# Row means on one core: the wait for the last store moved behind the closing barriers, waits reordered, and rows in three parts

## Chip, cores and metric

One core of a Trainium2 chip. The metric is the time of one execution in device microseconds (us). The span of a profile is the stretch from the kernel's first to its last instruction on any engine; the timed run is longer than its span.

## The reference

```python
batch, seq, dim = 32, 512, 1024          # x: float32, 67.1 MB
def reference(x, divisor):               # divisor = 1024.0
    return (np.sum(x, axis=-1) / divisor).astype(np.float32)
```

16,384 rows of 1,024 floats, one mean for each. On 128 partitions that makes 128 rows per partition.

## The kernel before

The rows lie in two parts. Of the first, each partition has 120 rows that follow one another in memory (so the next partition's block starts 480 KB further on); of the second, 8 rows (32 KB further on). The parts set which means go out with which store.

```python
L = 8
M = J - L                                                # 120
x_main = bass.AP(tensor=x.tensor, offset=0, ap=[[M * D, P], [D, M], [1, D]])
x_last = bass.AP(tensor=x.tensor, offset=P * M * D, ap=[[L * D, P], [D, L], [1, D]])
...
main = [(14, 0)] * 6 + [(14, 4), (14, 6), (8, 4)]        # (rows of a load, of them on ScalarE)
last = [(4, 2), (2, 1)]                                  # then one row, and one row in three pieces
bulk = ctx.enter_context(tc.tile_pool(name="bulk", bufs=3))
...
for rows, on_act in main:
    t = bulk.tile([P, 14, D], F32, name="t")
    load(t[:, :rows, :], x_main[:, j : j + rows, :])     # SyncE's queue
    sums(res[:, j : j + rows], t, rows, on_act)          # VectorE, a few rows on ScalarE
    j += rows
```

The last row is read in pieces pa, pb and pc, so that little arithmetic is left after the last byte:

```python
act_sum(pc[:, D - b : D - b + 1], pa)                    # ScalarE
nc.vector.reduce_sum(out=pc[:, D - b + 1 :], in_=pb, axis=AX)
nc.vector.reduce_sum(out=q[:, L - 1 :], in_=pc, axis=AX)
nc.vector.scalar_tensor_tensor(out=fin, in0=q, scalar=scale, in1=r, op0=MULT, op1=ADD)
tc.keep_in_program_order(nc.sync.dma_start(out=o_last, in_=fin))     # the last store
```

Behind it the program closes: SyncE waits for every engine and every DMA, and then all engines go through two barriers with a clearing of the semaphores between them.

Of the kernel before, what the change touches and what calls it, by code (L numbers as in the profile page):

```python
# [1 line left out]

# [4 lines left out]

F32 = mybir.dt.float32
ADD = mybir.AluOpType.add
MULT = mybir.AluOpType.mult  # L10
COPY = mybir.ActivationFunctionType.Copy
AX = mybir.AxisListType.X


def start_loads_at_once(nc):



    sp = mybir.EngineType.SP
    first, body = nc.main_func.blocks[0], nc.main_func.blocks[1]  # L20
    loads = []
    for i in body.instructions:
        if i.engine == sp:
            if type(i).__name__ != "InstDMACopy" or (i.sync_info and i.sync_info.on_wait):
                break
            loads.append(i)
    names = {i.name for i in loads}
    assert names
    body.instructions = [i for i in body.instructions if i.name not in names]
    at = next(  # L30
        k for k, i in enumerate(first.instructions) if i.engine == sp and type(i).__name__ == "InstDrain"
    )
    first.instructions = first.instructions[:at] + loads + first.instructions[at:]


@with_exitstack
def kernel(
    ctx: ExitStack,
    tc: tile.TileContext,
    x: bass.AP,  # L40
    divisor: float,
    out: bass.AP,
):
    nc = tc.nc
    nc.at_finalize(start_loads_at_once)
    xf = x.flatten_outer_dims()
    N, D = xf.shape
    P = nc.NUM_PARTITIONS
    scale = 1.0 / float(divisor)
    J = N // P  # L50
    assert J * P == N


    L = 8
    M = J - L
    x_main = bass.AP(tensor=x.tensor, offset=0, ap=[[M * D, P], [D, M], [1, D]])
    x_last = bass.AP(tensor=x.tensor, offset=P * M * D, ap=[[L * D, P], [D, L], [1, D]])
    o_main = bass.AP(tensor=out.tensor, offset=0, ap=[[M, P], [1, M]])
    o_last = bass.AP(tensor=out.tensor, offset=P * M, ap=[[L, P], [1, L]])


    main = [(14, 0)] * 6 + [(14, 4), (14, 6), (8, 4)]
    last = [(4, 2), (2, 1)]
    assert sum(n for n, _ in main) == M and sum(n for n, _ in last) == L - 2
    bulk = ctx.enter_context(tc.tile_pool(name="bulk", bufs=3))
    one = ctx.enter_context(tc.tile_pool(name="one", bufs=1))
    psum = ctx.enter_context(tc.tile_pool(name="junk", bufs=4, space=bass.MemoryType.PSUM))

    res = one.tile([P, M], F32, name="res")
    fin = one.tile([P, L], F32, name="fin")  # L70
    q = one.tile([P, L], F32, name="q")
    r = one.tile([P, L], F32, name="r")
    nc.gpsimd.memset(r, 0.0)  # L73

    def load(dst, src):
        tc.keep_in_program_order(nc.sync.dma_start(out=dst, in_=src))  # L76

    def act_sum(dst, src, by=1.0):
        n = src.shape[-1]
        junk = psum.tile([P, D], F32, name="junk")  # L80
        nc.scalar.activation(junk[:, :n], src, COPY, scale=by, accum_out=dst)  # L81

    def sums(dst, t, rows, on_act):
        d = rows - on_act
        for i in range(d, rows):
            act_sum(dst[:, i : i + 1], t[:, i, :])
        nc.vector.reduce_sum(out=dst[:, :d], in_=t[:, :d, :], axis=AX)  # L87

    j = 0
    for rows, on_act in main:  # L90
        t = bulk.tile([P, 14, D], F32, name="t")
        load(t[:, :rows, :], x_main[:, j : j + rows, :])
        sums(res[:, j : j + rows], t, rows, on_act)
        j += rows
    j = 0
    for rows, on_act in last:
        t = one.tile([P, rows, D], F32, name=f"t{rows}")
        load(t, x_last[:, j : j + rows, :])
        sums(q[:, j : j + rows], t, rows, on_act)
        j += rows  # L100


    c = 768
    row = one.tile([P, D], F32, name="row")
    load(row, x_last[:, j, :])
    act_sum(r[:, j : j + 1], row[:, c:], by=scale)
    nc.vector.reduce_sum(out=q[:, j : j + 1], in_=row[:, :c], axis=AX)  # L107



    a, b = 448, 704
    pa = one.tile([P, a], F32, name="pa")
    pb = one.tile([P, b - a], F32, name="pb")
    pc = one.tile([P, D - b + 2], F32, name="pc")
    load(pa, x_last[:, L - 1, :a])
    load(pb, x_last[:, L - 1, a:b])
    load(pc[:, : D - b], x_last[:, L - 1, b:])


    nc.gpsimd.tensor_scalar_mul(out=res, in0=res, scalar1=scale)  # L120
    tc.keep_in_program_order(nc.sync.dma_start(out=o_main, in_=res))

    act_sum(pc[:, D - b : D - b + 1], pa)
    nc.vector.reduce_sum(out=pc[:, D - b + 1 :], in_=pb, axis=AX)  # L124
    nc.vector.reduce_sum(out=q[:, L - 1 :], in_=pc, axis=AX)  # L125
    nc.vector.scalar_tensor_tensor(out=fin, in0=q, scalar=scale, in1=r, op0=MULT, op1=ADD)  # L126
    tc.keep_in_program_order(nc.sync.dma_start(out=o_last, in_=fin))


# [1 line left out]
_INS = ['x', 'divisor']  # L131
_OUTS = [((32, 512), 'float32')]

_NUMBERS = {'divisor': 1024.0}


# [26 lines left out]
```

## Time and profile before

| | |
|---|---|
| timed, median of 3 runs | 162.98 us (medians of five later sets: 162.89 to 163.01) |
| span of the profiled run | 161.51 us (its own time 163.29) |
| DMA engines full | 97.1% of the span |
| VectorE busy | 74% |
| first load's landing | 19.90 us |
| VectorE's last instruction ends | 159.14 us |
| last store's landing | 160.58 us |

The prediction below shows the lines of the page, of the stretches and of the end. How to read them: a stretch line has the window, then each engine's busy time with its number of instructions, then the DMA share and GB/s; a timeline line has start, duration, engine, line, operation and shapes. The closing itself can be seen in the view of the line that all closing instructions carry. Its columns are line, engine's queue, instruction and count, duration in ns (least, median, most), first and last start:

```profile
L158 SPq EVENT_SEMAPHORE  x7: 17/28/912, 159.6 to 161.4; - x7
L158 PEldq EVENT_SEMAPHORE  x2: 51/51/51, 161.0 to 161.5; - x2
```

SyncE stands for 912 ns in one wait (for the store's landing); only then TensorE's queue, which like all has one wait per barrier, passes the first at 161.0 and the second at 161.5.

### The profile page before, as it was taken

To read this page: it belongs to the slowest core of one execution; us is meant where nothing else is said; L and a number is where in the kernel's file an instruction comes from. 1 tells how busy PE (TensorE), PEld (TensorE's weight loads), DVE (VectorE), ACT (ScalarE), POOL (GpSimd) and SP (SyncE) were. 2 spreads that over 40 slices of the span, in tenths; PEclk is the share of its full clock that TensorE was granted. 3 is DMA by queue.
4 is the path that set the end of the run, shared out by engine and by line. 5 is a ranking of instruction groups with operands and counts; after the bars stand their busy time and mean duration, and the time that the engine had idled before them with its cause. 6 is when DMAs were issued, how large, how long until landed. Compare 5 with 4: busy or idle time off the path is not lost.

```text
span 161.5 us, 138 instructions
## 1 busy us (share of the span) xinstructions
DVE 120.0 (74%) x15; ACT 20.7 (13%) x39; POOL 0.8 (0%) x6
## 2 busy tenths in 40 slices
DVE  0000099968998699959995999599968970697893
ACT  3000000000000000000000000000008100682881
POOL 0000000000000000000000000000000000000100
DMA  9999999999989999999999899999999978999990
GB/s 298 398 440 454 454 454 454 454 440 440 412 355 398 454 454 454 454 454 454 440 440 412 355 398 454 454 454 454 454 454 440 440 327 383 487 414 394 410 384 6
DMA packets 2448, 67.18 MB, mean 416 GB/s; under 512 B 528, under 2 KB 912, under 8 KB 1040
## 3 DMA queue, kind: packets, MB, share of 16 engines
q1 hardware_dynamic: 2448, 67.18, 97.1%
HBM read 67.11 MB, written 0.07 MB: 416 GB/s over the span
## 4 chain that ended last, share of the span: by engine, by line
DMA 67%; DVE 29%; another core or an unknown queue 1%; SPq 1%; issue 0%; DVEq 0%
DMA t<-in_x_dram 45%; DVE res L87 28%; DMA row<-in_x_dram 22%; SPq L76 1%; DVE q L107 1%; DVE q L125 0%; DVE pc L124 0%; DVE fin L126 0%; DVEq L125 0%; DVEq L126 0%
## 5 line engine op out<-in xcount | busy, mean ns | idle before, releaser
L87 DVE TENSOR_REDUCE res<-t 128x14 f32<-128x14336 f32 (+3 forms) x9 | 114.4, 12716 | 38.2 <-DMA t<-in_x_dram 38.2
L81 ACT ACTIVATE junk<-t 128x1024 f32<-128x1024 f32 x17 | 17.2, 1013 | 135.6 <-DMA t<-in_x_dram 135.6
L87 DVE TENSOR_REDUCE q<-t 128x2 f32<-128x2048 f32 (+1 forms) x2 | 3.5, 1752 | 0.7 <-DMA t<-in_x_dram 0.7
L81 ACT ACTIVATION_READ_ACCUMULATOR junk<-t 128x1 f32 x17 | 3.2, 188 | 0.0
L81 ACT ACT_TABLE_LOAD x1 | 1.3, 1283 | 1.7 <-PEq L144 1.7
L120 POOL TENSOR_SCALAR res<-res 128x120 f32<-128x120 f32 x1 | 0.5, 513 | 151.0 <-DVE res L87 151.0
L107 DVE TENSOR_REDUCE q<-row 128x1 f32<-128x768 f32 x1 | 1.0, 953 | 0.1
L125 DVE TENSOR_REDUCE q<-pc 128x1 f32<-128x322 f32 x1 | 0.5, 489 | 0.1
L81 ACT ACTIVATE junk<-pa 128x448 f32<-128x448 f32 x1 | 0.5, 547 | 0.1
L124 DVE TENSOR_REDUCE pc<-pb 128x1 f32<-128x256 f32 x1 | 0.4, 420 | 0.0
L81 ACT ACTIVATE junk<-row 128x256 f32<-128x256 f32 x1 | 0.4, 388 | 0.2 <-DMA row<-in_x_dram 0.2
L126 DVE SCALAR_TENSOR_TENSOR fin<-q,r 128x8 f32<-128x8 f32 x1 | 0.2, 167 | 0.1
L81 ACT ACTIVATION_READ_ACCUMULATOR junk<-row 128x1 f32 x1 | 0.2, 188 | 0.0
L81 ACT ACTIVATION_READ_ACCUMULATOR junk<-pa 128x1 f32 x1 | 0.2, 185 | 0.0
L73 POOL MEMSET r<- 128x8 f32 x1 | 0.1, 105 | 1.3 <-POOLq L144 1.3
L144 POOL MEMSET const-bfloat16-1.0<- 128x1 bf16 x1 | 0.1, 102 | 0.0
L144 POOL MEMSET const-uint8-127<- 128x1 uint8 x1 | 0.1, 102 | 0.0
L144 POOL MEMSET const-float32-0.0<- 128x1 f32 x1 | 0.1, 99 | 0.2 <-issue 0.2
L144 POOL MEMSET const-float32-1.0<- 128x1 f32 x1 | 0.1, 100 | 0.0
## 6 DMA issues: line engine op xcount, KB each, us to landing
t<-in_x_dram SPq DMA_DIRECT2D x8, 7168.0 KB, 35.7
t<-in_x_dram SPq DMA_DIRECT2D x1, 4096.0 KB, 28.5
t<-in_x_dram SPq DMA_DIRECT2D x1, 2048.0 KB, 33.0
t<-in_x_dram SPq DMA_DIRECT2D x1, 1024.0 KB, 35.0
row<-in_x_dram SPq DMA_DIRECT2D x1, 512.0 KB, 35.9
pa<-in_x_dram SPq DMA_DIRECT2D x1, 224.0 KB, 36.0
pc<-in_x_dram SPq DMA_DIRECT2D x1, 160.0 KB, 35.7
pb<-in_x_dram SPq DMA_DIRECT2D x1, 128.0 KB, 35.8
```

What stands on the lines that cost most here:

```text
L73: nc.gpsimd.memset(r, 0.0)
L76: tc.keep_in_program_order(nc.sync.dma_start(out=dst, in_=src))
L81: nc.scalar.activation(junk[:, :n], src, COPY, scale=by, accum_out=dst)
L87: nc.vector.reduce_sum(out=dst[:, :d], in_=t[:, :d, :], axis=AX)
L107: nc.vector.reduce_sum(out=q[:, j : j + 1], in_=row[:, :c], axis=AX)
L120: nc.gpsimd.tensor_scalar_mul(out=res, in0=res, scalar1=scale)
L124: nc.vector.reduce_sum(out=pc[:, D - b + 1 :], in_=pb, axis=AX)
L125: nc.vector.reduce_sum(out=q[:, L - 1 :], in_=pc, axis=AX)
L126: nc.vector.scalar_tensor_tensor(out=fin, in0=q, scalar=scale, in1=r, op0=MULT, op1=ADD)
L144: nc = _bacc.Bacc("TRN2", target_bir_lowering=False, num_devices=1)
```

## The change

Three things. The last store is taken out of the body and put behind the wait that collects everything else, but ahead of the barriers; SyncE waits for its landing as the very last thing (with a semaphore of its own, which the clearing leaves alone). The prediction calls this "store behind the barriers"; it is the wait for the landing that goes behind them. Where an instruction waits for several semaphores, the one expected last is kept on the instruction itself. And the rows lie in three parts of 56, 56 and 16 rows per partition, so that a partition's block is 224 KB or 64 KB from the next; the first part's means get a store of their own in the middle of the loads.

```diff
+def latest_wait_first(nc):
+    def rank(i, w):
+        own = {"DVE": "DVE_", "Activation": "Activation_", "SP": "DVE_", "Pool": "DVE_"}
+        if w.ant_name.startswith("DMAHW") and i.engine != SP:
+            return 0
+        return 1 if w.ant_name.startswith(own.get(str(i.engine).split(".")[-1], "?")) else 2
+    ...                                   # sorts the waits of each body instruction by rank
+def close_while_storing(nc, landed):
+    ...
+    needs[lane.id] = ...                  # the collected wait no longer counts the last store
+    del needs[done.id]                    # nor VectorE's last instruction
+    last = nc.sync.wait_ge(landed, 16).ins
+    body.instructions = [i for i in body.instructions if i.name != store.name]
+    end.instructions = [
+        with_sync(drain, on_wait=tuple(needs.values())),
+        with_sync(store, on_wait=(done,), on_update=(add,)),
+        *end.instructions[1:-1],          # the two barriers and the clearing
+        with_sync(last, on_update=(sub,)),
+    ]
...
-    L = 8
-    M = J - L
+    B, L = 56, 16
...
-    main = [(14, 0)] * 6 + [(14, 4), (14, 6), (8, 4)]
-    last = [(4, 2), (2, 1)]
+    main = [[(14, 0)] * 4, [(14, 0)] * 2 + [(14, 4), (14, 6)]]
+    last = [(8, 4), (4, 2), (2, 1)]
...
+            if k == 1 and j == B:
+                means_out(0)              # scale and store the first part's means
```

More of the change, by code (lines that the diff above doesn't have):

```diff
@@ L1 @@
+import copy
+import dataclasses
 from contextlib import ExitStack
@@ L12 @@
 AX = mybir.AxisListType.X
+SP = mybir.EngineType.SP
 def start_loads_at_once(nc):
-    sp = mybir.EngineType.SP
     first, body = nc.main_func.blocks[0], nc.main_func.blocks[1]
@@ L22, in start_loads_at_once @@
     for i in body.instructions:
-        if i.engine == sp:
+        if i.engine == SP:
             if type(i).__name__ != "InstDMACopy" or (i.sync_info and i.sync_info.on_wait):
@@ L30, in start_loads_at_once, with with_sync @@
     at = next(
-        k for k, i in enumerate(first.instructions) if i.engine == sp and type(i).__name__ == "InstDrain"
+        k for k, i in enumerate(first.instructions) if i.engine == SP and type(i).__name__ == "InstDrain"
     )
     first.instructions = first.instructions[:at] + loads + first.instructions[at:]
+def with_sync(i, on_wait=None, on_update=None):
+    s = i.sync_info
+    return copy.replace(
+        i,
+        sync_info=mybir.SyncInfo(
+            on_wait=s.on_wait if on_wait is None else on_wait,
+            on_update=s.on_update if on_update is None else on_update,
+        ),
+    )
@@ new lines, in latest_wait_first @@
+def latest_wait_first(nc):
[4 more added lines that the diff above has]
+        return 1 if w.ant_name.startswith(own.get(str(i.engine).split(".")[-1], "?")) else 2
+    for block in nc.main_func.blocks[1:2]:
+        block.instructions = [
+            with_sync(i, on_wait=tuple(sorted(i.sync_info.on_wait, key=lambda w: rank(i, w))))
+            if i.sync_info and len(i.sync_info.on_wait) > 1
+            else i
+            for i in block.instructions
+        ]
@@ new lines, in close_while_storing @@
+def close_while_storing(nc, landed):
+    body, end = nc.main_func.blocks[1], nc.main_func.blocks[-1]
+    store = [i for i in body.instructions if i.engine == SP and type(i).__name__ == "InstDMACopy"][-1]
+    (lane,) = store.sync_info.on_update
+    drain = end.instructions[0]
+    assert drain.engine == SP and type(drain).__name__ == "InstDrain"
+    needs = {w.id: w for w in drain.sync_info.on_wait}
+    assert needs[lane.id].wait_value > lane.update_value
+    needs[lane.id] = dataclasses.replace(
+        needs[lane.id], wait_value=needs[lane.id].wait_value - lane.update_value
+    )
+    (done,) = [w for w in store.sync_info.on_wait if w.ant_name.startswith("DVE_")]
+    assert needs[done.id].wait_value == done.wait_value
+    del needs[done.id]
+    own = dict(sync_type="semaphore", id=landed.num, ant_name=landed.name)
+    add = mybir.SyncUpdate(update_mode="sem-add-imm", update_value=16, **own)
+    sub = mybir.SyncUpdate(update_mode="sem-sub-imm", update_value=16, **own)
+    last = nc.sync.wait_ge(landed, 16).ins
+    assert nc.main_func.blocks[-1].instructions[-1].name == last.name
+    body.instructions = [i for i in body.instructions if i.name != store.name]
[4 more added lines that the diff above has]
+        with_sync(last, on_update=(sub,)),
+    ]
@@ L44 @@
     nc = tc.nc
+    landed = nc.alloc_semaphore("landed")
     nc.at_finalize(start_loads_at_once)
+    nc.at_finalize(latest_wait_first)
+    nc.at_finalize(lambda nc: close_while_storing(nc, landed))
     xf = x.flatten_outer_dims()
@@ L51, with part @@
     assert J * P == N
-    L = 8
-    M = J - L
-    x_main = bass.AP(tensor=x.tensor, offset=0, ap=[[M * D, P], [D, M], [1, D]])
-    x_last = bass.AP(tensor=x.tensor, offset=P * M * D, ap=[[L * D, P], [D, L], [1, D]])
-    o_main = bass.AP(tensor=out.tensor, offset=0, ap=[[M, P], [1, M]])
-    o_last = bass.AP(tensor=out.tensor, offset=P * M, ap=[[L, P], [1, L]])
-    main = [(14, 0)] * 6 + [(14, 4), (14, 6), (8, 4)]
-    last = [(4, 2), (2, 1)]
-    assert sum(n for n, _ in main) == M and sum(n for n, _ in last) == L - 2
+    B, L = 56, 16
+    assert 2 * B + L == J
+    def part(t, first, n, width):
+        cols = [[width, n], [1, width]] if width > 1 else [[1, n]]
+        return bass.AP(tensor=t.tensor, offset=first * P * width, ap=[[n * width, P]] + cols)
+    x_part = [part(x, 0, B, D), part(x, B, B, D), part(x, 2 * B, L, D)]
+    o_part = [part(out, 0, B, 1), part(out, B, B, 1), part(out, 2 * B, L, 1)]
+    main = [[(14, 0)] * 4, [(14, 0)] * 2 + [(14, 4), (14, 6)]]
+    last = [(8, 4), (4, 2), (2, 1)]
+    assert all(sum(n for n, _ in m) == B for m in main) and sum(n for n, _ in last) == L - 2
     bulk = ctx.enter_context(tc.tile_pool(name="bulk", bufs=3))
@@ L67 @@
     psum = ctx.enter_context(tc.tile_pool(name="junk", bufs=4, space=bass.MemoryType.PSUM))
-    res = one.tile([P, M], F32, name="res")
+    res = [one.tile([P, B], F32, name=f"res{k}") for k in range(2)]
     fin = one.tile([P, L], F32, name="fin")
@@ L87, in sums, with means_out @@
         nc.vector.reduce_sum(out=dst[:, :d], in_=t[:, :d, :], axis=AX)
-    j = 0
-    for rows, on_act in main:
-        t = bulk.tile([P, 14, D], F32, name="t")
-        load(t[:, :rows, :], x_main[:, j : j + rows, :])
-        sums(res[:, j : j + rows], t, rows, on_act)
-        j += rows
+    def means_out(k):
+        nc.gpsimd.tensor_scalar_mul(out=res[k], in0=res[k], scalar1=scale)
+        tc.keep_in_program_order(nc.sync.dma_start(out=o_part[k], in_=res[k]))
+    for k in range(2):
+        j = 0
+        for rows, on_act in main[k]:
+            t = bulk.tile([P, 14, D], F32, name="t")
+            load(t, x_part[k][:, j : j + rows, :])
+            sums(res[k][:, j : j + rows], t, rows, on_act)
+            j += rows
+            if k == 1 and j == B:
+                means_out(0)
     j = 0
     for rows, on_act in last:
-        t = one.tile([P, rows, D], F32, name=f"t{rows}")
-        load(t, x_last[:, j : j + rows, :])
+        if rows == 8:
+            t = bulk.tile([P, 14, D], F32, name="t")[:, :8, :]
+        else:
+            t = one.tile([P, rows, D], F32, name=f"t{rows}")
+        load(t, x_part[2][:, j : j + rows, :])
         sums(q[:, j : j + rows], t, rows, on_act)
@@ L104 @@
     row = one.tile([P, D], F32, name="row")
-    load(row, x_last[:, j, :])
+    load(row, x_part[2][:, j, :])
     act_sum(r[:, j : j + 1], row[:, c:], by=scale)
@@ L114 @@
     pc = one.tile([P, D - b + 2], F32, name="pc")
-    load(pa, x_last[:, L - 1, :a])
-    load(pb, x_last[:, L - 1, a:b])
-    load(pc[:, : D - b], x_last[:, L - 1, b:])
-    nc.gpsimd.tensor_scalar_mul(out=res, in0=res, scalar1=scale)
-    tc.keep_in_program_order(nc.sync.dma_start(out=o_main, in_=res))
+    load(pa, x_part[2][:, L - 1, :a])
+    load(pb, x_part[2][:, L - 1, a:b])
+    load(pc[:, : D - b], x_part[2][:, L - 1, b:])
+    means_out(1)
     act_sum(pc[:, D - b : D - b + 1], pa)
@@ L126 @@
     nc.vector.scalar_tensor_tensor(out=fin, in0=q, scalar=scale, in1=r, op0=MULT, op1=ADD)
-    tc.keep_in_program_order(nc.sync.dma_start(out=o_last, in_=fin))
+    tc.keep_in_program_order(nc.sync.dma_start(out=o_part[2], in_=fin))
 _INS = ['x', 'divisor']
```

## The prediction

> **What bounds the kernel now.** The kernel sums 16,384 rows of 1,024 floats, so it reads 67.1 MB and does one pass of adds. I read the head of the page first (who is busy), then the stretches of the run (is the transfer rate steady), then the chain and the timeline of the last microseconds, then what SyncE's queue waits for at the end.
>
> The page, busy shares and DMA queue:
>
> ```profile
> DVE 120.0 (74%) x15; ACT 20.7 (13%) x39; POOL 0.8 (0%) x6
> ...
> q1 hardware_dynamic: 2448, 67.18, 97.1%
> ```
>
> The 16 DMA engines are 97.1% full, and VectorE has a quarter of the span free. Stretches of one load each (columns: from:to, length, DVE, ACT, POOL, clock, DMA share, GB/s):
>
> ```profile
> 20.00:37.00 17.00, 15.18 (x2) 0.00 (x0) 0.00 (x0) 1.00 1.00 432
> 37.00:54.00 17.00, 15.14 (x2) 0.00 (x0) 0.00 (x0) 1.00 1.00 432
> 105.00:122.00 17.00, 15.14 (x2) 0.46 (x1) 0.00 (x0) 1.00 1.00 432
> 122.00:138.50 16.50, 10.37 (x2) 3.81 (x8) 0.00 (x0) 1.00 0.98 421
> 138.50:158.30 19.80, 17.97 (x6) 15.14 (x30) 0.51 (x1) 1.00 0.95 400
> ```
>
> Every stretch moves 432 GB/s until the short pieces of the end. (The coarse strip of 40 slices wavers between 355 and 454 only because a 57,344-byte packet falls into one slice or the next.) In the trace's packets, one of 57,344 bytes takes 2,116 ns at the median, so 16 engines move 16 x 57,344 / 2,116 = 433.6 GB/s. The exception is the first packet of each engine: 2,333 to 3,552 ns. The slowest engine finishes its first one at 4.76 us, and seven more at 2.116 us each end at 19.6, which agrees with the first landing at 19.90. The loads then land at 36.81, 53.76 and so on, 16.94 us apart (8 x 2.116 = 16.93). So what the slowest engine loses in its first packet is never won back, and afterwards nothing is lost.
>
> The end, timeline from 156.5 us:
>
> ```profile
> 156.93 0.95 DVE L107 TENSOR_REDUCE q<-row 128x1 f32<-128x768 f32 x1
> 157.87 0.42 DVE L124 TENSOR_REDUCE pc<-pb 128x1 f32<-128x256 f32 x1
> 158.07 0.18 ACT L81 ACTIVATION_READ_ACCUMULATOR junk<-pa 128x1 f32 x1
> 158.38 0.49 DVE L125 TENSOR_REDUCE q<-pc 128x1 f32<-128x322 f32 x1
> 158.98 0.17 DVE L126 SCALAR_TENSOR_TENSOR fin<-q,r 128x8 f32<-128x8 f32 x1
> 159.17 0.34 SPq L127 DMA_DIRECT2D out_dram<-fin  x1
> ```
>
> and what SyncE waits for after it, with the time of that store to landing:
>
> ```profile
> SPq L158 <- DMA out_dram<-fin: 0.9, 1, 0.9
> ```
> ```profile
> out_dram<-fin SPq DMA_DIRECT2D x1, 4.0 KB, 1.4
> ```
>
> The last piece pc lands at 158.25; VectorE ends pb's sum at 158.29 and ScalarE pa's at 158.25, so three legs meet. The store is issued at 159.17 and its last semaphore increment comes at 160.58. Only then does SyncE go through its remaining waits and the two closing barriers, to the end at 161.51. The tail from 158.25 to 161.51 is 3.26 us: 0.92 arithmetic, 1.41 store, 0.93 closing.
>
> **What the Trainium skill says.** "DMA: Bandwidth & Descriptors", section Specifications, gives 435 GB/s as the fabric ceiling; the 433.6 above agrees, so the steady state has no headroom for a new address pattern to win. The same page, "Latency and other measured facts", row "HBM row pitch at large powers of two", tells of pitches of 512 KiB and more that slow copies (207 GB/s at 512 KiB, 103 at 4 MiB); the 480 KB pitch of this kernel shows no such loss after the first packets, and 224 and 64 KB are not in its list. The same page's "Anatomy of one DMA" puts most of a small DMA's fixed time of about 2 us into the receipt of the write, not the moving; here the 4 KB store needs 1.41 us although its packets take 7 to 9 ns each, so it is latency that other work can cover. "Perfetto Trace Analysis", section Identifying Dependency Chains, says that an instruction with several waits may have semaphore instructions put before it; the trace has such a one at 158.28 ahead of the reduction of pc and at 158.91 ahead of the last multiply-add.
>
> **The change part by part.** From the built order of both kernels: the loads keep number, sizes and order; VectorE and ScalarE have the same instructions on the same shapes (fin is 16 wide in place of 8). Four things differ.
>
> 1. *Store behind the barriers.* SyncE makes its collected waits first, without VectorE's last and without this store; then it issues the store, takes part in both barriers, and waits for the landing last. Are its collected waits met in time? The last are pc's landing (158.25) and the landing of the store of the earlier means (158.50 in the trace); some waits at about 0.06 us each (159.56, 159.62, 159.69 are the starts of three in a row) follow, so SyncE is ready near 158.8, before VectorE's end at 159.14. After the issue at 159.17 + 0.34 = 159.51 the barriers take what they take now, from SyncE's drain at 160.76 to 161.51, 0.75 us: to about 160.3. The landing at 160.58 is later and decides; with some 0.05 us for the wait itself the end is at 160.63. Saved: 161.51 - 160.63 = 0.88 us.
>
> 2. *Order of waits.* The instruction now keeps the wait expected last and the others stand in the one before it. For the reduction of pc, all three legs end within 0.04 us and the separate instruction still has VectorE's and ScalarE's, so nothing is gained. For the last multiply-add, Pool's wait is long met and it waits for VectorE alone: 158.87 to 158.98 may shrink by some 0.05 us. Saved: 0.05.
>
> 3. *Three parts.* One more store of 28 KB enters the rings between the 8th and the 9th load: 8 packets of 224 bytes and a semaphore packet on each engine. Packets of 32 bytes take 9 ns, of 480 take 26, so about 16 for 224: 8 x 16 + 9 = 0.14 us ahead of all later data. The packets of the second store (8 x 26 ns to 8 x 16) lie behind pc and off the path. The load of pc now waits in SyncE's queue for the 8th load's landing, at 138.5 in place of 122.5 us; 19 us of data are still queued ahead of it, so this costs nothing. Cost: 0.14.
>
> 4. *Pitch of 224 and 64 KB.* It can act only where engines are slower than 2,116 ns: in the first packets, 0.2 to 1.4 us above it. If the pitch causes the spread, at best the slowest engine gains about 0.9 us (4.76 to 3.85, the end of the fastest). [...]I take a third, 0.3 us; this term is a choice.
>
> Sum: -0.88 - 0.05 + 0.14 - 0.30 = -1.09, so 162.98 - 1.09 = 161.89 us.
>
> **The rivals.**
> - *Barrier in place of the landing.* If the closing takes longer than 1.07 us from the store's issue (0.75 now), or SyncE's collected waits run past 159.14, the gain of part 1 shrinks to about 0.5 and the time is 162.3. For it: SyncE's margin is only about 0.3 us and the store of the earlier means lands late. Against: the measured pieces are short.
> - *The pitch matters at the start.* Then all of 0.9 us comes and the time is about 161.3. For it: the spread of the first packets, at the only moment when all 16 engines walk in step. Against: the move from 480 KB to 32 KB pitch within the kernel leaves no mark (16,384-byte packets take 608 to 621 ns).
> - *The new pitch aliases.* If 224 KB made packets slow as large powers of two do, even 3% of 155 us is 4.6 us and the time 167.6. Against: 224 KB is no power of two; 64 KB is one, but serves only 16 of 128 rows.
> - *The gain is outside what is timed.* The timed 162.98 is 1.5 us above the profiled span of 161.5. If something after the span waited for the store anyway, almost nothing would be gained: 162.9. I think it unlikely, as the store's landing is still waited for inside the program.
>
> **Range and chances.** The rivals lie at 161.3, 162.3 and 162.9 around 161.9; the runs of before spread by 0.3. Eight in ten: 161.0 to 162.6. Faster by over 2% needs under 159.7, 3.3 us less; parts 1, 2 and the whole of 4 make 1.8, so 2%. Slower by over 2% needs 166.2, only through aliasing: 2%. The rest, 96%, is within 2%.
>
> **What would show it.** Right: the last store stands ahead of the barriers, some 1.4 us before its landing, and the span ends under 0.1 us after it; VectorE's last idle before the multiply-add is about 0.05 us shorter; stretches in the middle still carry 432 GB/s; the first landing moves from 19.90 to about 19.6. Wrong: a first landing at 19.0 or at 20.5 (part 4 mis-sized); later landings not 16.94 us apart (aliasing); a gap between the landing of the earlier means' store and the last store's issue (SyncE late); a span shorter by 0.9 while the timed runs don't move.

## The result, and the profile after

The changed kernel took 161.95 us (median of 4, 161.80 to 162.01) against 162.94 us (median of 4). A ratio here is the mean time of one kernel's fast runs over that of the other's of the same rounds, so not quite the ratio of the medians: 0.9937, 95% interval 0.9920 to 0.9954. A later set gave 161.72 against 162.89, 0.9926 (0.9914 to 0.9939). So 1.0 to 1.2 us were gained, 0.6 to 0.7%; 161.89 had been predicted.

Stretches of the changed kernel:

```profile
20.00:37.00 17.00, 15.17 (x2) 0.00 (x0) 0.00 (x0) 1.00 1.00 432
105.00:122.00 17.00, 15.14 (x2) 0.39 (x1) 0.00 (x0) 1.00 1.00 432
138.50:158.30 19.80, 17.96 (x7) 15.12 (x30) 0.35 (x1) 1.00 0.94 394
```

The middle is the same 432 GB/s; nothing aliases. The end of the timeline:

```profile
158.23 0.49 DVE L204 TENSOR_REDUCE q<-pc 128x1 f32<-128x322 f32 x1
158.76 0.17 DVE L205 SCALAR_TENSOR_TENSOR fin<-q,r 128x16 f32<-128x16 f32 x1
158.96 0.34 SPq L206 DMA_DIRECT2D out_dram<-fin  x1
```

and what SyncE waited for there (total, times, longest), with the closing's instructions:

```profile
SPq L206 <- DVE fin L205: 0.5, 1, 0.5
SPq L88 <- SPq L88: 0.3, 1, 0.3
```
```profile
L237 PEldq EVENT_SEMAPHORE  x2: 51/51/51, 159.6 to 160.1; - x2
L88 SPq EVENT_SEMAPHORE  x1: 17/17/17, 160.4 to 160.4; - x1
```

SyncE is ready half a microsecond before VectorE's last instruction ends, so its collected waits are no obstacle. Both barriers are through at 160.17 while the store is still on its way; SyncE then waits 0.3 us for the landing, and the span ends at 160.40, 0.03 us after it. That was 0.93 us before.

The span fell by 1.11 us (161.51 to 160.40), but the profiled run of before was one of its slowest; of nine other runs of before the spans are 161.1 to 161.3. Against those the span fell by 0.8 to 0.9. The rest is in a place the prediction hadn't looked at: the timed run exceeds its span by 1.74 to 1.84 us before and by 1.50 to 1.60 after.

### The profile page after: what moved, and what is told of

It is laid out like the page before. It is cut to its first block, busy times and chain, and to the rows that moved or that the text cites. A ratio compares the mean times of both kernels' runs of the same rounds, so it can differ in the third digit from the quotient of the medians.

```text
span 160.4 us, 140 instructions
## 1 busy us (share of the span) xinstructions
DVE 119.9 (75%) x15; ACT 20.7 (13%) x39; POOL 1.0 (1%) x7
## 4 chain that ended last, share of the span: by engine, by line
DMA 67%; DVE 30%; another core or an unknown queue 1%; SPq 1%; issue 0%; DVEq 0%
DMA t<-in_x_dram 67%; DVE res L157 28%; DVE q L157 1%; SPq L146 1%; DVE q L187 1%; DVE q L204 0%; DVE pc L203 0%; DVE fin L205 0%; DVEq L204 0%
## 5 line engine op out<-in xcount | busy, mean ns | idle before, releaser
L157 DVE TENSOR_REDUCE res<-t 128x14 f32<-128x14336 f32 (+2 forms) x8 | 110.0, 13753 | 37.2 <-DMA t<-in_x_dram 37.2
L157 DVE TENSOR_REDUCE q<-t 128x4 f32<-128x4096 f32 (+2 forms) x3 | 7.9, 2642 | 1.6 <-DMA t<-in_x_dram 1.5
L160 POOL TENSOR_SCALAR res<-res 128x56 f32<-128x56 f32 x2 | 0.7, 352 | 145.2 <-DVE res L157 145.2
```

What stands on the lines that cost most here:

```text
L157: nc.vector.reduce_sum(out=dst[:, :d], in_=t[:, :d, :], axis=AX)
L160: nc.gpsimd.tensor_scalar_mul(out=res[k], in0=res[k], scalar1=scale)
```

## The experiments

Twelve more sets ran, with five rounds asked for each; where only four came back, the text says so. First-landing times, and the ends of barriers, are read from the records of semaphores in the trace. "Tail" is from the 9th load's landing to pc's. "Barriers" is the end of the last barrier's last wait; "SyncE" the end of SyncE's last instruction; both, and the time, of the profiled run itself.

| kernel | median | ratio to before (95%) | first landing | tail | barriers | SyncE | time | time - barriers | time - SyncE |
|---|---|---|---|---|---|---|---|---|---|
| before | | | 19.90 | 10.02 | 161.51 | 161.46 | 163.29 | 1.78 | 1.83 |
| changed | 161.95 | 0.9937 (0.9920 to 0.9954) | 19.95 | 9.79 | 160.17 | 160.40 | 161.95 | 1.78 | 1.55 |
| close_only | 161.88 | 0.9931 (0.9918 to 0.9943) | 19.46 | 10.06 | 159.94 | 160.17 | 161.72 | 1.78 | 1.55 |
| order_only | 162.97 | 0.9997 (0.9985 to 1.0010) | 19.42 | 10.06 | 161.00 | 160.95 | 162.78 | 1.78 | 1.83 |
| parts_only | 163.20 | 1.0007 (0.9993 to 1.0021) | 19.78 | 9.90 | 161.77 | 161.72 | 163.55 | 1.78 | 1.83 |
| close_order | 161.84 | 0.9930 (0.9917 to 0.9942) | 19.68 | 10.05 | 160.03 | 160.26 | 161.82 | 1.79 | 1.56 |
| changed_again | 161.72 | 0.9926 (0.9914 to 0.9939) | 19.73 | 9.87 | 159.96 | 160.19 | 161.75 | 1.79 | 1.56 |
| late_store | 161.73 | 0.9927 (0.9914 to 0.9941) | 19.88 | 9.87 | 160.08 | 160.31 | 161.86 | 1.78 | 1.55 |
| five_stores | 162.46 | 0.9979 (0.9967 to 0.9992) | 19.93 | 9.84 | 160.65 | 160.88 | 162.44 | 1.79 | 1.56 |
| late_issue | 162.60 | 0.9980 (0.9968 to 0.9993) | 19.95 | 9.81 | 159.82 | 161.28 | 162.60 | 2.78 | 1.32 |
| join_first | 161.94 | 0.9934 (0.9921 to 0.9946) | 19.97 | 9.90 | 159.90 | 160.61 | 161.94 | 2.04 | 1.33 |
| two_parts | 161.32 | 0.9895 (0.9882 to 0.9909) | 19.41 | 9.74 | 159.52 | 159.74 | 161.30 | 1.78 | 1.56 |
| tail_32 | 162.15 | 0.9944 (0.9931 to 0.9958) | 19.98 | 10.04 | 160.45 | 160.68 | 162.23 | 1.78 | 1.55 |
| two_parts_join | 161.28 | 0.9893 (0.9876 to 0.9909) | 19.31 | 10.26 | 159.75 | 160.46 | 161.78 | 2.03 | 1.32 |

**First set: the change taken apart.** Four kernels on one chip, each with some of the three things.

*close_only*: the kernel before with close_while_storing alone.

```diff
+    landed = nc.alloc_semaphore("landed")
     nc.at_finalize(start_loads_at_once)
+    nc.at_finalize(lambda nc: close_while_storing(nc, landed))
```

> The layout and the wait order of before, with the last store behind the closing barriers. Theory A (the landing is covered by the closing; the two traces give 0.90 us for it): 0.90 us under before, ratio 0.9945, the span ending under 0.1 us after the store's last increment. Rival B (the closing barriers or SyncE's collected waits take its place): at most 0.5 us under before, and a gap between the store's landing and the end, or the store issued later than 0.05 us after VectorE's end.

Measured: 161.88 against 163.01 us, 1.13 us less (0.9931). More than theory A's 0.90, and all of the change's gain. VectorE's last instruction in its profile, and the closing (from its end at 158.70 to the end of the last barrier at 159.94 are 1.24 us, where the kernel before has 2.37):

```profile
158.54 0.17 DVE L192 SCALAR_TENSOR_TENSOR fin<-q,r 128x8 f32<-128x8 f32 x1
```
```profile
L224 PEldq EVENT_SEMAPHORE  x2: 51/51/51, 159.4 to 159.9; - x2
L89 SPq EVENT_SEMAPHORE  x1: 17/17/17, 160.2 to 160.2; - x1
```

*order_only*: the kernel before with latest_wait_first alone.

```diff
     nc.at_finalize(start_loads_at_once)
+    nc.at_finalize(latest_wait_first)
```

> The kernel before with the order of waits alone changed. Theory A: 0.07 us under before (ratio 0.9996), seen as the gap between the reduction of pc and the last multiply-add falling from 0.10 to 0.03 us; the gap before the reduction of pc stays near 0.10 us. Rival: waiting on the late semaphore directly saves 0.05 us at each landing, so that all legs of the end move and 0.2 us are gained (0.9988).

Measured: 162.97 us, 0.04 less, inside the noise (0.9985 to 1.0010). The timeline has the mechanism:

```profile
157.94 0.49 DVE L190 TENSOR_REDUCE q<-pc 128x1 f32<-128x322 f32 x1
158.46 0.17 DVE L191 SCALAR_TENSOR_TENSOR fin<-q,r 128x8 f32<-128x8 f32 x1
```

From the first line's end (157.94 + 0.49 = 158.43) to the second's start are 0.03 us, where the kernel before has 158.98 - 158.87 = 0.10 (its reduction runs from 158.38 for 0.49). Waiting before the reduction of pc is unchanged: it starts 0.10 us after pb's sum ends at 157.84, as before. So 0.07 us on the path are gained, as theory A has it; the runs are too coarse to confirm it in time.

*parts_only*: the changed kernel without the other two.

```diff
-    landed = nc.alloc_semaphore("landed")
     nc.at_finalize(start_loads_at_once)
-    nc.at_finalize(latest_wait_first)
-    nc.at_finalize(lambda nc: close_while_storing(nc, landed))
```

> The three parts with their pitches alone; store, barriers and waits as before. Theory A: what is left over of the 1.1 us, 0.1 to 0.2 us under before (0.9990), from the stretch after 122 us, not from the first landing, which stays at 19.9 to 19.95. Rival B (the pitch speeds up the first packets): first landing under 19.7 and 0.3 us or more gained (0.9980). Rival C (the pitch does nothing and the store in the middle costs its packets): 0.14 us over before (1.0009).

Measured: 163.20 against 163.01 us, the interval including no change (0.9993 to 1.0021). Theory A's gain of 0.1 to 0.2 us isn't there, and rival B's neither; it lies nearest to rival C, which late_store below tests. Its profiled execution was the slowest of the five (163.55; the others 162.96 to 163.21), with the 6th to 8th loads landing 17.02 to 17.16 us apart in place of 16.94, so I read no more from that trace.

*close_order*: the first two together in the layout of before.

```diff
+    landed = nc.alloc_semaphore("landed")
     nc.at_finalize(start_loads_at_once)
+    nc.at_finalize(latest_wait_first)
+    nc.at_finalize(lambda nc: close_while_storing(nc, landed))
```

> Store behind the barriers and the order of waits, in the layout of before. Theory A: 0.97 us under before (0.9940), so 0.1 to 0.2 us over the changed kernel. Rival C (the layout costs its extra store): 1.0 us under before and level with or faster than the changed kernel (0.9937 or less).

Measured: 161.84 us, 1.17 less (0.9930), where rival C would have it, and level with the changed kernel's 0.9937 and 0.9926. So the three parts, taken as a whole, are worth nothing that these runs can see, and the closing is worth 1.13 instead of 0.90 us. Two questions: where do 0.23 us more come from, and what do the parts do inside?

**Second set: what the closing really waits for, and the store in the middle.** The table's last columns raise the first question's answer: in every kernel of the first set the time is 1.78 or 1.79 us after the last barrier, while "after SyncE's end" has two values. If that is a rule, the landing isn't what sets the time. *late_issue* pulls the two apart:

```diff
-    del needs[done.id]
     ...
         with_sync(drain, on_wait=tuple(needs.values())),
-        with_sync(store, on_wait=(done,), on_update=(add,)),
         *end.instructions[1:-1],
+        with_sync(store, on_wait=(), on_update=(add,)),
         with_sync(last, on_update=(sub,)),
```

(SyncE's collected wait includes VectorE's last instruction again, so the store needs no wait of its own.) It ran together with *changed_again*, the changed kernel unaltered, which came 1.17 us under before (0.9926, where 0.9937 was expected):

> The changed kernel once more, on the chip of the next three, as their measure. Both theories: 0.99 to 1.0 us under before (0.9937), the timed run 1.54 us over its span where before has 1.80.

> The changed kernel with the last store issued after the closing barriers and not before them, so that SyncE ends about 0.8 us later and the other engines have ended long before it. It asks what the 0.26 us are that the timed run gained beyond its span. Theory A (SyncE's own end sets the time, and what follows its last instruction takes 1.54 us): the timed run is again 1.54 us over the span, 0.8 us over the changed kernel. Rival (in the changed kernel the other engines' exits, 1.80 us after the last barrier, set the time): the timed run is less than 1.5 us over the span, so less is lost than the span grows by.

Measured: 162.60 us, 0.88 over changed_again. The closing of its profile, with the store, in the same views as above (the last line is SyncE's wait for the landing):

```profile
159.83 0.34 SPq L205 DMA_DIRECT2D out_dram<-fin  x1
```
```profile
L236 PEldq EVENT_SEMAPHORE  x2: 51/51/51, 159.3 to 159.8; - x2
L87 SPq EVENT_SEMAPHORE  x1: 17/17/17, 161.3 to 161.3; - x1
```

The barriers are over at 159.82, SyncE at 161.28, and the time is 1.32 us after SyncE, not 1.55: theory A (as this expectation numbered it) falls and the rival holds. The reading that fits is that the end comes 1.78 us after the last barrier or 1.32 us after SyncE's last instruction, whichever is later; join_first and two_parts_join below bear it out. What runs in these 1.78 us lies behind the profile and isn't shown. In the changed kernel the barriers give 160.17 + 1.78 = 161.95 and the landing 160.40 + 1.32 = 161.72. The barriers set the time, 0.23 us ahead of the landing.

*late_store* moves the store in the middle to the end of the loads:

```diff
-            if k == 1 and j == B:
-                means_out(0)
...
+    means_out(0)
     means_out(1)
```

> The changed kernel with the store of the first part's means moved from the middle to just before the store of the second part's, behind all loads. Theory A (the store in the middle costs the ring time of its packets): 0.14 us under the changed kernel, the gap between the landings of the 8th and 9th load down from 9.78 to 9.64 us. Rival (the pitches of 224 and 64 KB cost it): no gain, within 0.05 us of the changed kernel.

Measured: 161.73 us, level with changed_again's 161.72. The gap between the 8th and the 9th landing is 9.72 us, and 9.67 to 9.76 in the seven kernels without that store (9.76 in the kernel before, at most 9.72 in the others), against 9.75 to 9.80 in six kernels with it. So the expected 0.14 is 0.03 at the landings against changed_again and 0.06 between the medians of the two groups, which touch, and it is not to be seen in the time.

*five_stores* cuts that store in five:

```diff
-        tc.keep_in_program_order(nc.sync.dma_start(out=o_part[k], in_=res[k]))
+        step = 12 if k == 0 else B
+        for a in range(0, B, step):
+            b = min(a + step, B)
+            tc.keep_in_program_order(nc.sync.dma_start(out=o_part[k][:, a:b], in_=res[k][:, a:b]))
```

> The changed kernel with the store in the middle cut into five of 12, 12, 12, 12 and 8 columns. Theory A: 5 x 8 packets of about 9.5 ns and 5 semaphore packets of 9 ns on each engine make 0.43 in place of 0.14 us, so 0.29 us over the changed kernel (ratio to before 0.9955), seen as a longer gap between the landings of the 8th and 9th load. Rival (stores cost no ring time beside the loads): no change.

Measured: 162.46 us, 0.74 over changed_again where 0.29 was expected. Starts of the first, eighth and ninth load's sums:

```profile
19.95 15.09 DVE L157 TENSOR_REDUCE res<-t 128x14 f32<-128x14336 f32 x1 [19.95 <-DMA t<-in_x_dram]
138.83 8.69 DVE L157 TENSOR_REDUCE res<-t 128x8 f32<-128x8192 f32 x1 [6.43 <-DMA t<-in_x_dram]
148.82 4.42 DVE L157 TENSOR_REDUCE q<-t 128x4 f32<-128x4096 f32 x1 [1.31 <-DMA t<-in_x_dram]
```

The same of changed_again, which ran beside it:

```profile
19.75 15.09 DVE L157 TENSOR_REDUCE res<-t 128x14 f32<-128x14336 f32 x1 [19.75 <-DMA t<-in_x_dram]
138.35 8.69 DVE L157 TENSOR_REDUCE res<-t 128x8 f32<-128x8192 f32 x1 [6.18 <-DMA t<-in_x_dram]
148.10 4.42 DVE L157 TENSOR_REDUCE q<-t 128x4 f32<-128x4096 f32 x1 [1.07 <-DMA t<-in_x_dram]
```

From first to eighth are 118.88 us (138.35 - 19.75 = 118.60 in changed_again), from eighth to ninth 9.99 (148.10 - 138.35 = 9.75): 0.28 and 0.24 us more, 0.52 in all. The eighth load's data is not later: from the first landing to the end of its last packet are 118.14 us, 118.13 in changed_again. Only its last semaphore increment comes later, 0.74 us after that packet's end in place of 0.47. Then 28 of the ninth load's 128 packets take more than 1,230 ns, up to 1,829, where none does in changed_again (median 1,213 in both). What else the two profiled executions differ by (162.44 against 161.75) is the first landing, 19.93 against 19.73, before any store; how the 0.74 between the medians divides, no run shows. Counting packets by their own time mis-sizes a small store in both directions: one was cheaper than counted, and five cost more at the landings (0.52 where 0.29 was counted).

**Third set: the layout's two faces.** All eight profiles with 224 KB for the first load land it at 19.73 to 19.98 us; the four with 480 KB at 19.42 to 19.90. In each of the eight at least one engine begins its first packet late, the last of them at 1.78 to 2.69 us; in the four of 480 KB none begins after 1.64. In seven of the eight this engine is also the last to finish its first packet (in tail_32 another is). A late start isn't the only way to a late landing: in the kernel before, which landed at 19.90, the slowest engine began at 1.22 and took 3.55 us. On the other side, the tail is 9.74 to 9.90 us with the 64 KB pitch in undisturbed profiles and 10.02 to 10.06 with 32 KB. (These counts include the kernels below.) *two_parts* keeps the 64 KB and drops the 224:

```diff
-    B, L = 56, 16
-    assert 2 * B + L == J
+    B, L = 112, 16
+    assert B + L == J
...
-    main = [[(14, 0)] * 4, [(14, 0)] * 2 + [(14, 4), (14, 6)]]
+    main = [[(14, 0)] * 6 + [(14, 4), (14, 6)]]
```

> The changed kernel with two parts of 112 and 16 rows (pitches 448 and 64 KB), so without the store in the middle. Theory A (in six profiles of the 224 KB pitch one engine started its first packet 0.5 to 1.6 us late, in four of 480 KB none did by more than 0.6; and the 64 KB pitch saves 0.2 us in the last loads): no engine's first packet starts after 1.7 us, the first landing is under 19.7, the stretch from the 9th landing to pc's is 9.8 to 9.87 us, and the time is 0.2 us under the changed kernel (0.992). Rival (the spread of the first packets is chance and the layout does nothing): first landing anywhere from 19.4 to 19.95 and the time within 0.1 us of the changed kernel (0.9925 to 0.994).

Measured: 161.32 us (median of 4; 0.9895), 0.5 to 0.7 us under the changed kernel by the ratio of this set and its two; its interval (0.9882 to 0.9909) touches neither of the changed kernel's. The three starts and the end:

```profile
19.43 15.09 DVE L157 TENSOR_REDUCE res<-t 128x14 f32<-128x14336 f32 x1 [19.43 <-DMA t<-in_x_dram]
147.72 4.42 DVE L157 TENSOR_REDUCE q<-t 128x4 f32<-128x4096 f32 x1 [1.03 <-DMA t<-in_x_dram]
157.58 0.49 DVE L202 TENSOR_REDUCE q<-pc 128x1 f32<-128x322 f32 x1
158.31 0.34 SPq L204 DMA_DIRECT2D out_dram<-fin  x1
```

The first sum starts 0.55 us earlier than in the changed kernel (19.98), and that is kept to the end: the last store starts 0.65 earlier (158.31 against 158.96). No engine's first packet starts after 1.37 us. Theory A holds for the first packets, with a gain larger than it said; the tail, 9.74 us, is below the 9.8 to 9.87 that it gave.

*tail_32* goes the other way: parts of 56, 64 and 8 rows, so that the last loads are 32 KB apart again.

```diff
-    B, L = 56, 16
+    B, C, L = 56, 64, 8
...
-    main = [[(14, 0)] * 4, [(14, 0)] * 2 + [(14, 4), (14, 6)]]
-    last = [(8, 4), (4, 2), (2, 1)]
+    main = [[(14, 0)] * 4, [(14, 0)] * 2 + [(14, 4), (14, 6), (8, 4)]]
+    last = [(4, 2), (2, 1)]
```

> The changed kernel with parts of 56, 64 and 8 rows (pitches 224, 256 and 32 KB), so that the last loads have the pitch of the kernel before. Theory A (the last loads gain by the 64 KB pitch): 10.02 to 10.06 us from the 9th landing to pc's, as in the four profiles of the layout of before, and 0.2 us over the changed kernel (0.9945). Rival (it comes from something else, as the late issue of pc): 9.8 to 9.87 us and the time of the changed kernel.

Measured: a tail of 10.04 us and 0.9944, as theory A says. Its ninth sum and that of pc:

```profile
148.37 4.42 DVE L157 TENSOR_REDUCE res<-t 128x4 f32<-128x4096 f32 x1 [1.11 <-DMA t<-in_x_dram]
158.52 0.49 DVE L204 TENSOR_REDUCE q<-pc 128x1 f32<-128x322 f32 x1
```

From 148.37 to 158.52 are 10.15 us, where two_parts has 9.86. pc is issued late (after the 8th landing) in this kernel too, so that isn't the reason. Nor can it be only the store of the earlier means, which the kernels of 32 KB issue at 152.8 to 153.4 us and those of 64 KB at 147.3 to 148.2: the load of four rows lands before the later store is issued and already comes 4.87 to 4.92 us after the ninth at 32 KB (five profiles), 4.82 to 4.84 at 64 KB (nine). That is a third of the difference; for the rest this rival isn't excluded. The packets of 16,384 bytes take 611 to 613 ns at the median at 32 KB and 611 at 64; what makes their landings follow faster at 64 KB I can't say from the packets' own times. It stays open, as does why one engine begins late at 224 KB.

*join_first* makes use of the 0.23 us by which the landing is early: SyncE joins the first barrier before it issues the store.

```diff
-    del needs[done.id]
+    needs = {done.id: needs[done.id], **{k: w for k, w in needs.items() if k != done.id}}
...
-        with_sync(store, on_wait=(done,), on_update=(add,)),
-        *end.instructions[1:-1],
+        *end.instructions[1 : joined + 1],          # up to SyncE's step into the first barrier
+        with_sync(store, on_wait=(), on_update=(add,)),
+        *end.instructions[joined + 1 : -1],
```

> The changed kernel with SyncE waiting for VectorE and joining the first closing barrier before it issues the last store; the rest of the closing stands behind the store. The store starts some 0.1 us later and the last barrier ends some 0.4 us earlier. Theory A (the time is the later of two: the last barrier plus 1.80 us, SyncE's last instruction plus 1.29 us or less): 0.18 us under the changed kernel, ratio to before 0.9915 to 0.992, the timed run about 1.3 us over the span, and the span 0.1 us longer. Rival (the time is SyncE's end plus 1.54 us): 0.1 us over the changed kernel, the timed run still 1.54 over the span.

Measured: 161.94 us (0.9934), no gain in time, so that size was a miss. The mechanism is there: the time is 1.33 us after SyncE's end and no longer 1.55. Counted from the end of VectorE's last instruction (158.93 in the changed kernel, 159.00 here), the last barrier came after 0.90 in place of 1.24 us, but the landing after 1.57 in place of 1.44 us, and so the time after 2.94 in place of 3.02: 0.08 us better, not 0.18. The expectation had the store only 0.10 us later (it was 0.14: 0.17 after VectorE's end in place of 0.03) and SyncE's last piece at 1.29 us (it was 1.33), and this execution's first landing was a late one, 19.97 us. The later start of the store can be seen against VectorE's end (158.82 + 0.18 = 159.00), and the barriers and SyncE's last wait in the closing's view:

```profile
158.82 0.18 DVE L207 SCALAR_TENSOR_TENSOR fin<-q,r 128x16 f32<-128x16 f32 x1
159.16 0.34 SPq L208 DMA_DIRECT2D out_dram<-fin  x1
```
```profile
L239 PEldq EVENT_SEMAPHORE  x2: 51/51/51, 159.2 to 159.8; - x2
L89 SPq EVENT_SEMAPHORE  x1: 17/17/17, 160.6 to 160.6; - x1
```

**Last run: the two put together.** *two_parts_join* is two_parts with the edit of join_first.

> The two parts of 112 and 16 rows together with SyncE joining the first closing barrier before it issues the last store: the best of both. Theory A (the layout gains by the first packets and the 64 KB pitch, the closing is the later of the last barrier plus 1.80 and SyncE's end plus 1.31 us; joining first is worth 0.09 us counted from VectorE's last instruction): first landing under 19.7 and no first packet after 1.7 us again, 9.70 to 9.87 us from the 9th landing to pc's, the timed run 1.3 to 1.4 us over the span, and 161.2 to 161.35 us (0.989 to 0.990). Rival (the two-part run was a lucky draw of the first packets): first landing at 19.7 to 20.0 and 161.6 us or more (0.992).

Measured: 161.28 us (median of 4), 0.9893. The first landing is 19.31 us again, so two_parts was no lucky draw; one engine began its first packet at 1.83 us, which theory A had excluded, without being the last to finish it. The profiled execution was a disturbed one (161.78; the other three 161.21 to 161.32): its 8th load took 17.12 in place of 16.95 us and the load of the single row landed 1.73 in place of 1.24 us after the one before, which also accounts for its tail of 10.26. That the undisturbed runs are 0.07 us under two_parts (161.25 against 161.32, on another chip) is too little to be called shown. This or two_parts is the best version found, 1.6 to 1.7 us under before and 0.5 to 0.7 under the change.

## Why the prediction was right or wrong

The number was right: 161.89 predicted, 161.95 and 161.72 measured, within 2% as said. But of its four terms the first was a quarter of a microsecond too small, the third and fourth together promised 0.16 us that did not come, and these errors nearly cancelled: that the number came within 0.2 us is in part luck.

1. *Store behind the barriers, 0.88 us: the part inside the span was right, the rule that set the end was not.* From landing to the span's end fell from 0.93 to 0.03 us, so 0.90 in the span. (After the issue the barriers took 0.87 us where 0.75 was counted, 159.30 to 160.17, still ahead of the landing.) But close_only measured 1.13. The step that failed is "the landing at 160.58 is later and decides": it decides the span, while the time is decided by the last barrier plus 1.78 us, 0.23 us later than the landing would have it. Counted from VectorE's last instruction the last barrier came at 161.51 - 159.14 = 2.37 us before and at 160.17 - 158.93 = 1.24 after: 1.13 us; in close_only's profile it is 1.24 too, and its gain was 1.13 (0.93 to 1.34 by its interval). The first rival, the barrier in place of the landing, named what then set the end, but with the wrong sign: it expected a smaller gain from it, because it compared the barriers with the landing and not with where the barriers had been before. The last rival, that the gain might vanish outside the span, had the right place and again the wrong sign: about 0.25 us more came from there (1.8 us over the span became 1.55).
2. *Order of waits, 0.05 us: right.* 0.07 us in the trace before the last multiply-add and none before pc's reduction. In the time not separable from zero.
3. *Store in the middle, +0.14 us: too large.* 0.03 to 0.06 at the landings, nothing in late_store's time. The count of packets was right (16 ns each, as estimated), the inference from packets to time wasn't, as five_stores showed from the other side.
4. *Pitch, -0.30 us: wrong in its place.* The first landing didn't move to 19.6: the engine that lands last was mostly later with 224 KB (19.73 to 19.98 in eight profiles) than with 480 (19.42 to 19.90 in four). The prediction took the one landing of 19.90 for the kernel's own, and three more profiles of that layout had 19.42 to 19.68. (The fastest engine ended its first packet at 3.81, not 3.85, which changes nothing.) What the pitch did give was where the prediction had said it leaves no mark, the last loads: about 0.2 us from 64 in place of 32 KB (medians 9.86 and 10.05). Both together are near zero: close_order and the changed kernel are level.

Aliasing, the one way to a slower kernel, didn't happen: landings follow one another by 16.94 us before and after.

## What to carry to other kernels

A last store's latency can lie beside the closing barriers if the wait for it is the last thing in the program; what then counts, as here, can be when the last barrier ends and no longer when the store lands, so look at the time minus the span in every run, not at the span alone. Try the distance between partitions' blocks on the first landing and on the last loads separately, since one layout here gained at one end what it lost at the other, and the one that gained at both (448 and 64 KB) was simpler than the change. And when a sum comes out right, test its terms.

## What the Trainium skill lacked or had wrong

- "Runtime: NRT & Kernel Launch", section The ~15µs preamble/postamble breakdown, lists the steps after the kernel one after another (barrier about 1.5, semaphore reset about 1.5, barrier and re-arming about 2 us). It doesn't say what has to have ended before they begin. Here the time ends 1.78 us after the last barrier of the engines, or 1.32 us after SyncE's last instruction, whichever is later (eleven profiles of the first kind, three of the second). Which step the difference of 0.46 us is, no run shows.
- "DMA: Bandwidth & Descriptors", Latency and other measured facts, row "HBM row pitch at large powers of two": begins at 512 KiB (207 GB/s, beside 214 at full rate in the same row) and tells of lasting rates. It has nothing on the start of a stream (slowest engine's first landing 19.73 to 19.98 us at 224 KB, 19.42 to 19.90 at 480, 19.31 and 19.41 at 448) or on small pitches (last loads 10.02 to 10.06 us at 32 KB, 9.74 to 9.90 at 64 in undisturbed profiles).
- The same page's Specifications say that transfers under 512 B are read, modified and written, but not what a small store costs the loads beside it: one of 224-byte packets 0.03 to 0.06 us at the landings, five of 32 to 48 bytes in its place 0.52 us more.
- The same page's Anatomy of one DMA gives about 2 us as the fixed time of a DMA on the gpsimd path, and the page has no such time for a store that SyncE issues; the last stores here, of 4 and 8 KB, take 1.40 to 1.42 us from the start of their issue to the last increment.
